# A short-convolution and pooling encoder layer on one core: the first upper gate tile loaded in whole rows and transposed on TensorE, and two tiles of the last pair exchanged in a ring of five

## Chip, core and metric

The kernel runs on one core of a Trainium2 chip, as one launch. The metric is device time in microseconds (us), lower is better. The core has five engines with instruction queues of their own, each worked through in order: PE (TensorE, matrix products; its weight loads are shown as PEld), DVE (VectorE), ACT (ScalarE), POOL (GpSimd) and SP (SyncE, which here only issues DMAs). POOL and ACT issue DMAs too.

## The reference

One layer of a streaming encoder in float32, for a prompt of 2048 frames and a sample of 32 frames, width 1024:

```python
def layer(h, p, conv_hist, pool_hist, pos, g_mix, w_in, conv_w, conv_b, pool_w, pool_scale,
          w_out, g_ple, w_ple_gate, w_ple):
    hn = rmsnorm(h, g_mix)
    proj = hn @ w_in                                             # 1024 x 3072
    hA, bA, cA, zA, vB, zB = jnp.split(proj, ..., axis=-1)       # 512 columns each
    yA, new_conv = short_conv_mixer(hA, bA, cA, zA, conv_hist, conv_w, conv_b)
    yB, new_pool = pooling_mixer(vB, zB, pool_hist, pos, pool_w, pool_scale)
    h = h + jnp.concatenate([yA, yB], axis=-1) @ w_out           # 1024 x 1024
    gate = jax.nn.sigmoid(rmsnorm(h, g_ple) @ w_ple_gate)        # 1024 x 1024
    h = h + (p @ w_ple) * gate                                   # p: 256 wide
    return h, new_conv, new_pool
# then a last rmsnorm(h, g_final)
```

The change lies in the last three of these lines: the gate product, the embedding product `p @ w_ple`, their product added to h, and the last norm.

## The kernel before

**Numbers.** A float32 operand is split into two parts, high and low (`split`: ACT casts the high part, DVE subtracts it), and a product is three PE passes of parts. Products of two tiles of 128 rows by the 1024 x 1024 weights are done in a scheme with seven half-size products instead of eight (`seven`): the operand is cut into quarters a11, a12, a21, a22, and sums of them ("frames" 11, 12, S1 to S4, 22) are multiplied by sums of the weight's quarters ("11", "T1" to "T4", "21", "22").

**Stages.** First the projection with the mixers (to about 523 us of the profile), then the product with `w_out` pair by pair of tiles (the o pairs; their results h go to DRAM as `h_d`), then the gate stage from about 705 us, which the change is in. There are 17 tiles: 16 of 128 rows and one of 32.

**The gate stage.** It begins with the late part of the embedding products (`embed`, tiles 7 to 14 and the short one; L109 and L137). For each of them SP loads an operand `pps` (256 KB), PE does two halves of six matmuls, ACT copies each half out of PSUM (`eout`, L167) and POOL stores it to `e_d`. PSUM has six banks for products (`ps_m`) and two for transposes (`ps_t`). Beside these products the weights of the gate are made into their sums (L195, L203, L210; loads `wg_b` from `g_d`), and the frames of the first pair are made (`prep_g`). Then come the eight gate pairs, `seven` for each: `carry` copies a partial product out (L1573), `out` adds, applies the sigmoid and multiplies with the tile e of `e_d` (L1579 to L1584); for most tiles POOL then adds h by an accumulating DMA (L1590); the finish (square L94, scaling L1597, store L1600) of one pair runs under the next one.

**How a tile of h gets its columns on the partitions.** The gate product needs h transposed. There are two ways. `by_quarters` loads a tile from `h_d` with four DMAs, each to 32 partitions in pieces of 1 KB, so that one DVE transpose within 32 x 32 blocks (`turned_here`, L1560) does the rest, in place; its callers pin that transpose in program order on DVE. `turned` takes a tile in whole rows, reorders its columns by two ACT copies into tiles of the ring `qa` (L1552), and transposes it by eight PE transposes into the two PSUM banks of `ps_t` (L1554); it pins nothing. Before the change only the short tile (32 rows) goes this way. Both tiles of the first pair, `first_lower` (tile 1) and `first_h` (tile 0, the upper one), are loaded by quarters. `first_h` is issued on SP behind the loads of the embedding weights (`wq`) and of the last two `wg_b`, and ahead of the `pps` of the fourth late tile and the ones after it. `prep_g(0)`'s step `second`, which makes all frames but the lower tile's, is traced behind the fifth late embedding product.

**The last pair** (`last_pair`, tiles 14 and 15) is ordered by hand: its steps are pinned with `keep_in_program_order`. Its tiles in the ring `ya` (five buffers) are one h (tile 15), one e (tile 14) and the two result tiles hg; the other h (tile 14) is in the ring `xh`, and tile 15's embedding product is made in place on PE (`e_l`). The finish of the pair before (`square1`, `scale1`, `square0`, `scale0`) runs in its steps.

**Order.** The program is traced once; a planner then orders the instructions of each engine by priority (program order) and by the time at which its own plan has them ready, gives tiles their buffers in a ring as these become free in the plan, and sets the semaphores. `keep_in_program_order` pins an instruction behind the one traced before it on its engine; `issue_after` puts a block's instructions behind a given one on its engine.

Of the kernel before, what the change touches and what calls it, by code (L numbers as in the profile page):

```python
# [36 lines left out]
def trunk(ctx, tc, x_p, x_s, c_conv, c_pool, p_p, p_s, g_mix, w_in, conv_w, conv_b, pool_w,  # L37
# [8 lines left out]
    h_d = tc.dram_tile([T, D], F32, name="h_d")  # L46
    e_d = tc.dram_tile([T, D], F32, name="e_d")
# [11 lines left out]
    def tbank(name):  # L59
        return ps_t.tile([P, 512], F32, tag="tr", name=name)  # L60
# [19 lines left out]
    def split(hi, lo, src, eng=nc.vector, later=False):  # L80
        ins = nc.scalar.copy(hi, src)  # L81
        if later:
            tc.keep_in_program_order(ins)
        eng.tensor_tensor(lo, src, hi.bitcast(F32), op=ALU.subtract)  # L84
        return ins
# [17 lines left out]
    def rows_of(pr, sa, r, n):  # L103
        return pr[r:r + n] if r < SEQ else sa
# [12 lines left out]
    def load_wp(pool, name, queue):  # L117
        wp = []
        for k in range(2):
            t = [pool.tile([P, KH, 2, P], F32R, tag="c", name=f"{name}_{k}_{h}").rearrange("p a b c -> p (a b c)")  # L120
                 for h in range(2)]
            for h in range(2):
                queue.dma_start(t[h].bitcast(F32), wl_d[k][h])
            wp.append(t)
        return wp

    def load_pps(t, i, queue, ins=False):
        n = 4 * tiles[i][1]
        load = queue.dma_start(t.rearrange("p a k n -> p (a k n)")[:, :n].bitcast(F32), pp_d[i, :, :n])
        return load if ins else t  # L130
# [251 lines left out]
    def ring4(t, name):  # L382
        return t.tile([P, D], F32, tag="t", name=name)
# [9 lines left out]
    def load_rows(pool, name, i, pr, sa=None, queue=nc.sync):  # L393
        r, n = tiles[i]
        t = ring4(pool, f"{name}_{i}")
        queue.dma_start(t[:n], pr[r:r + n] if sa is None else rows_of(pr, sa, r, n))
        return t

    with ExitStack() as s1:
# [58 lines left out]
        hn = {}  # L458
# [845 lines left out]
    with ExitStack() as s2:  # L1304
        pool = lambda name, bufs: s2.enter_context(tc.tile_pool(name=name, bufs=bufs, reuse_waits="tile"))
        qa, xh, ya, cmb = (pool(*a) for a in (("qa", 2), ("xh", 4), ("ya", 5), ("cmb", 8)))
# [79 lines left out]
        def rows_of_weight(pool, name, src, which, ks=range(KH)):  # L1386
            a = []
            for k in ks:
                a.append(ring4(pool, f"{name}_{k}") if pool is not cmb else cmb.tile([P, D], F32, tag="c", name=f"{name}_{k}"))
                ins = nc.sync.dma_start(a[-1], src[(which * KH + k) * P:(which * KH + k + 1) * P])  # L1390
            return a, ins
# [115 lines left out]
        def by_quarters(i, pool=ya):  # L1507

            r, n = tiles[i]
            t = ring4(xh if i > 3 else pool, f"hn_{i}")  # L1510
            for q in range(4):
                nc.sync.dma_start(t[q * 32:q * 32 + 32].rearrange("p (g c) -> p g c", g=4),
                                  h_d[r:r + P, q * 256:q * 256 + 256].rearrange("(g p) c -> p g c", p=32))
            return t
# [4 lines left out]
        got = {0: load_pps(ss.tile([P, 2, 2, P], F32R, tag="s", name=f"pps_{EARLY}"), EARLY, nc.sync)}  # L1519
# [8 lines left out]
            bots = rows_of_weight(cmb, "wg_b", g_d, 1, range(2))[0]  # L1528
        with tc.issue_after(embed_weight.ins):
            bots += rows_of_weight(cmb, "wg_b", g_d, 1, range(2, KH))[0]  # L1530
            first_h = by_quarters(0, xh)

        rest_e = [*range(EARLY, NT - 2), NT - 1]

# [9 lines left out]
        def turned(i, t=None):  # L1544

            r, n = tiles[i]
            t = (t or load_rows(ya, "hn", i, h_d)).rearrange("p (q k c) -> p k q c", q=4, k=KC)
            out = []
            for half in range(2):
                pt = tbank(f"pth_{i}_{half}")  # L1550
                o = qa.tile([P, KH, P], F32, tag="q", name=f"ho_{i}_{half}")
                nc.scalar.copy(o[:n].rearrange("p k (q c) -> p k q c", q=4), t[:n, half * KH:half * KH + KH])  # L1552
                for k in range(KH):
                    nc.tensor.transpose(pt[:, k * P:k * P + n], o[:n, k], ident[:n, :n])  # L1554
                out.append(pt.rearrange("p (k t) -> p k t", k=KH))
            return out

        def turned_here(t, pin=False):

            ins = nc.vector.transpose(t, t)  # L1560
            if pin:
                tc.keep_in_program_order(ins)
            u = t.rearrange("p (g k t) -> p k g t", g=4, k=KC)
            return u[:, :KH], u[:, KH:]
# [55 lines left out]
        def last_pair(i, A, square0, scale0, square1, scale1):  # L1620
# [6 lines left out]
            wp = []  # L1627
            chunk = lambda: wp.extend(load_wp(cmb, "wl", nc.sync))

            h = [load_rows(ya if b else xh, "h", i + b, h_d) for b in range(2)]  # L1630
            e = load_rows(ya, "e", i, e_d)
            tt = nc.vector.tensor_tensor
            carry, _ = gate_ops(h, [e], P, f"g{i}", i)
            hg = [ring4(ya, f"hg_{b}") for b in range(2)]
# [104 lines left out]
        def prep_g(i, ahead=False):  # L1739

            A, got = {}, {}
            whole = lambda t: t.rearrange("p k (g t) -> p k g t", g=4)

            def put(q, src, view=lambda t: t):
                A[q] = cmb.tile([P, KH, 2, P], F32R, tag="c", name=f"g{i}_{q}")
                split(view(A[q][:, :, 0]), view(A[q][:, :, 1]), src)

            def comb(q, x, y, op):
                t = whole(ss.tile([P, KH, P], F32, tag="s", name=f"g{i}_f{q}"))
                nc.vector.tensor_tensor(t, x, y, op=op)  # L1750
                return t

            lower = []

            def load():
                got["lower"] = by_quarters(i + 1) if i else first_lower
                got["upper"] = by_quarters(i) if i else first_h

            if ahead:
                load()  # L1760

            def sooner():
                if not ahead:
                    load()

            def first():
                if not got:
                    load()
                lower.extend(turned_here(got["lower"], True))

            def second():
                a21, a22 = lower
                s1 = comb("S1", a21, a22, ALU.add)
                a11, a12 = turned_here(got["upper"], True)
                put("11", a11, whole)
                s2 = comb("S2", s1, a11, ALU.subtract)
                s3 = comb("S3", a11, a21, ALU.subtract)
                put("12", a12, whole)
                put("S2", s2, whole)
                s4 = comb("S4", a12, s2, ALU.subtract)  # L1780
                put("S1", s1, whole)
                put("S3", s3, whole)
                put("S4", s4, whole)
                put("22", a22, whole)

            S[i] = A
            return {1: sooner, 2: first, 4 if i in (2, 8) else 3: second}
# [54 lines left out]
        for i in range(0, NT - 3, 2):  # L1842
            A = S.pop(i)
            following = prep_g(i + 2, not i)
            e = [load_rows(ya if i else xh, "e", i + b, e_d) for b in range(2)]
# [6 lines left out]
            if i in (0, 2, 4):  # L1852
                next(short_steps)
        last_pair(NT - 3, S[NT - 3], *finish)

# [27 lines left out]
```

## Time and profile before

| | us |
|---|---|
| median of three runs (911.08, 914.3, 911.03) | 911.08 |
| profiled execution, time | 913.21 |
| profiled execution, span of its instructions | 911.4 |
| PE busy | 889.4 |
| DVE busy | 696.0 |
| ACT busy | 452.6 |
| POOL busy | 166.8 |

The times of the table's last five rows come from one profiled execution. A row of the profile names the source line (L109 is line 109 of the kernel), the engine, the operation, what it writes and reads (`e<-wq,pps`) without buffer numbers, shapes, and a count. Rows of the timeline start with the start and the time that the merged instructions took; in brackets stands the idle time of the engine before them and what ended it. In the groups of instructions the times are least, median and largest in ns. For a DMA the first time is that of its issue; the time to its landing stands in the rows of DMA issues. Rows with SPq show the DMA queue of SP: what it issues and what it waits for. The profile's page notes that a wait for several semaphores is put down to the one that came last, and that this may be a wrong one where the engine named had long been done.

### The profile page before, as it was taken

What the parts mean: (1) busy time and instruction counts of PE and PEld (TensorE: products, weight loads), DVE (VectorE), ACT (ScalarE), POOL (GpSimd) and SP (SyncE); (2) the same over time, 40 slices, a digit from 0 to 9 for tenths busy, and PEclk for the clock granted to TensorE, in tenths of its full rate; (3) what the DMA queues carried; (4) which work ended last, traced back from release to release, by engine and by line L of the source; (5) the groups of instructions that cost most, each with busy time, mean ns of one, the idle gap of its engine ahead of it and who ended that gap; (6) DMA issues with size and microseconds to landing.
All of it is one profiled execution on the core that took longest, in us unless ns stands there. A gap on an engine that the chain in (4) does not pass through costs nothing. (4 is left out here: it accounts for less than half of the span.)

```text
span 911.4 us, 12057 instructions
## 1 busy us (share of the span) xinstructions
PE 889.4 (98%) x4110; PEld 717.0 (79%) x4110; DVE 696.0 (76%) x1140; ACT 452.6 (50%) x818; POOL 166.8 (18%) x303
## 2 busy tenths in 40 slices
PE   8999999999999999999999999999999899999996
PEld 6788888888888778877788886888887787777884
DVE  6899789897993687846767679956556967789775
ACT  7744555554453354533443365643435765446453
POOL 2210121222121023100000021211111201313322
PEclk9999999999999999999999999999999999999999
DMA  8255286857699676767744595778678784787875
GB/s 263 66 187 176 79 264 201 245 165 216 188 344 427 165 219 190 228 208 247 245 144 160 179 347 183 253 243 269 217 240 281 274 256 99 197 201 214 224 211 195
DMA packets 116843, 198.51 MB, mean 218 GB/s; under 512 B 13558, under 2 KB 74542, under 8 KB 115885
## 3 DMA queue, kind: packets, MB, share of 16 engines
q1 hardware_dynamic: 92893, 117.91, 41.1%
q0 software_dynamic: 21440, 75.44, 26.2%
q10 hardware_dynamic: 2448, 4.39, 1.3%
q8 instruction: 32, 0.52, 0.2%
q14 instruction: 30, 0.25, 0.1%
HBM read 132.53 MB, written 65.15 MB: 217 GB/s over the span
## 5 line engine op out<-in xcount | busy, mean ns | idle before, releaser
L185 PE MATMUL z_g<-wg,g_S 128*128 128x512 f32 x192 | 46.7, 392 | 2.1 <-ACT c_g L1573 2.1
L185 PE MATMUL z_o<-wo,y_S 128*128 128x512 f32 x192 | 47.4, 389 | 0.0
L185 PE MATMUL x_o<-wo_T,y_S 128*128 128x512 f32 x192 | 46.3, 390 | 0.7 <-DVE c_o L1319 0.7
L646 PE MATMUL x_zab<-B,w_zab_S 128*128 128x512 f32 x192 | 46.8, 392 | 0.2 <-DVE w_zab_S L84 0.2
L646 PE MATMUL z_zab<-B,w_zab_S 128*128 128x512 f32 x192 | 46.8, 391 | 0.0
L185 PE MATMUL x_o<-wo,y 128*128 128x512 f32 x192 | 45.2, 389 | 0.0
L185 PEld LDWEIGHTS z_g<-wg,g_S 128*128 128x128 f32 x192 | 35.7, 188 | 11.0 <-ACT c_g L1573 3.7
L646 PEld LDWEIGHTS x_zab<-B,w_zab_S 128*128 128x128 f32 x192 | 35.8, 188 | 8.9 <-DVE w_zab_S L84 0.6
L185 PEld LDWEIGHTS x_o<-wo_T,y_S 128*128 128x128 f32 x192 | 35.9, 188 | 8.6 <-DVE c_o L1319 1.2
L185 PEld LDWEIGHTS x_o<-wo,y 128*128 128x128 f32 x192 | 36.0, 188 | 7.7
L646 PEld LDWEIGHTS z_zab<-B,w_zab_S 128*128 128x128 f32 x192 | 35.8, 188 | 7.9 <-DVE w_zab_S L84 0.3
L185 PEld LDWEIGHTS z_o<-wo,y_S 128*128 128x128 f32 x192 | 36.0, 188 | 7.5
L646 PE MATMUL x_ch<-B,w_ch_S 128*128 128x512 f32 x168 | 41.9, 392 | 0.0
L646 PE MATMUL x_zbv<-B,w_zbv_S 128*128 128x512 f32 x168 | 40.9, 392 | 0.5 <-ACT zs L986 0.5
L646 PE MATMUL z_zbv<-B,w_zbv_S 128*128 128x512 f32 x168 | 40.4, 390 | 0.0
L646 PE MATMUL z_ch<-B,w_ch_S 128*128 128x512 f32 x168 | 40.4, 389 | 0.0
L646 PEld LDWEIGHTS x_zbv<-B,w_zbv_S 128*128 128x128 f32 x168 | 31.3, 188 | 8.2 <-ACT zs L986 0.9
L646 PEld LDWEIGHTS x_ch<-B,w_ch_S 128*128 128x128 f32 x168 | 31.3, 188 | 7.3 <-ACT U L986 0.4
L646 PEld LDWEIGHTS z_ch<-B,w_ch_S 128*128 128x128 f32 x168 | 31.5, 188 | 6.6
L646 PEld LDWEIGHTS z_zbv<-B,w_zbv_S 128*128 128x128 f32 x168 | 31.5, 188 | 6.5
L81 ACT CAST y_S<-y_fS 128x512 fp32r<-128x512 f32 x28 | 17.0, 619 | 27.4 <-PE x_o L185 12.0
L1373 POOL DMA_DIRECT2D gs<-in_w_ple_gate_dram x16 | 11.5, 718 | 86.7 <-DMA g_d<-gs 48.4
(554 smaller groups left out, 2272.0 us busy)
## 6 DMA issues: line engine op xcount, KB each, us to landing
wn<-in_w_in_dram SPq DMA_DIRECT2D x24, 512.0 KB, 5.1
hn<-h_d SPq DMA_DIRECT2D x65, 128.0 KB, 6.5
y<-y_d SPq DMA_DIRECT2D x16, 512.0 KB, 6.2
p_dT<-T POOLq DMA_DIRECT2D x15, 512.0 KB, 5.1
e<-e_d SPq DMA_DIRECT2D x15, 512.0 KB, 7.0
x<-in_x_prompt_dram SPq DMA_DIRECT2D x14, 512.0 KB, 5.8
e<-h_d POOLq DMA_DIRECT2D x13, 512.0 KB, 8.3
B<-p_d POOLq DMA_DIRECT2D x3, 2048.0 KB, 15.5
```

Source lines behind the costliest of these rows:

```text
L81: ins = nc.scalar.copy(hi, src)
L185: nc.tensor.matmul(ps[:n], lhs[:, k, a, :n], w[b][:, k], start=start and k + q == 0, stop=k == KH - 1 and q == 2, skip_group_check=True)
L646: nc.tensor.matmul(ps, lhs[:, k, x], b[:, k, y], start=start and k + q == 0, stop=stop and k == KH - 1 and q == 2, skip_group_check=True)
L1373: ins = nc.gpsimd.dma_start(t, rows[:, :, half * NH:half * NH + NH])
```

## The change

Three places. The first upper tile is loaded by one DMA in whole rows (`load_rows`, still into the ring `xh`), and `prep_g(0)` transposes it by `turned` instead of `turned_here`; all other tiles of the pairs stay as they were. In `last_pair` the e tile is requested ahead of the two h tiles, so in the ring of five e takes the place that the second h had, and that h the next one.

```diff
         with tc.issue_after(embed_weight.ins):
             bots += rows_of_weight(cmb, "wg_b", g_d, 1, range(2, KH))[0]
-            first_h = by_quarters(0, xh)
+            first_h = load_rows(xh, "hn", 0, h_d)
...
             chunk = lambda: wp.extend(load_wp(cmb, "wl", nc.sync))

+            e = load_rows(ya, "e", i, e_d)
             h = [load_rows(ya if b else xh, "h", i + b, h_d) for b in range(2)]
-            e = load_rows(ya, "e", i, e_d)
...
                 s1 = comb("S1", a21, a22, ALU.add)
-                a11, a12 = turned_here(got["upper"], True)
+                a11, a12 = turned_here(got["upper"], True) if i else map(whole, turned(0, got["upper"]))
                 put("11", a11, whole)
```

`turned`, which is not changed:

```python
        def turned(i, t=None):

            r, n = tiles[i]
            t = (t or load_rows(ya, "hn", i, h_d)).rearrange("p (q k c) -> p k q c", q=4, k=KC)
            out = []
            for half in range(2):
                pt = tbank(f"pth_{i}_{half}")
                o = qa.tile([P, KH, P], F32, tag="q", name=f"ho_{i}_{half}")
                nc.scalar.copy(o[:n].rearrange("p k (q c) -> p k q c", q=4), t[:n, half * KH:half * KH + KH])
                for k in range(KH):
                    nc.tensor.transpose(pt[:, k * P:k * P + n], o[:n, k], ident[:n, :n])
                out.append(pt.rearrange("p (k t) -> p k t", k=KH))
            return out
```

## The prediction

> **What bounds the kernel now.** I read the busy times and the chain first, then the stretch in which the changed tile is used, then the last pair.
>
> ```profile
> PE 889.4 (98%) x4110; PEld 717.0 (79%) x4110; DVE 696.0 (76%) x1140; ACT 452.6 (50%) x818; POOL 166.8 (18%) x303
> ...
> PE x_g L185 2%; PE z_g L185 1%; DMA e<-e_d 1%; PE y_g L185 1%; DVE hn L1560 1%; DVE e L1597 1%; PE x_g L1722 0%; DVE g_fS L1750 0%; ACT c_g L1582 0%; DVE e L1584 0%; ACT g_S L81 0%; DVE g_S L84 0%; PE e_l L109 0%; DVE c_g L1581 0%; DVE g L84 0%
> ```
>
> PE is busy for 98%, so a change pays only where PE waits or runs slowly, or behind its last product. The chain names one transfer, the last pair's e. The table by stretches, around the place where the first upper tile is used, shows the other place:
>
> ```profile
> core 0: us, PE busy (x) PEld busy (x) DVE busy (x) ACT busy (x) POOL busy (x), PEclk, DMA share, GB/s
> ...
> 713.00:717.00 4.00, 1.30 (x6) 0.79 (x5) 4.00 (x8) 3.52 (x7) 0.93 (x2) 1.00 1.02 407
> 717.00:721.00 4.00, 4.00 (x12) 3.13 (x11) 4.00 (x7) 4.00 (x9) 0.04 (x1) 0.57 0.40 160
> ```
>
> From 713 to 717 PE worked 1.30 us of 4 while the DMA engines were full (share 1.02); in the next 4 us its granted clock averaged 0.57. The timeline has the two costs:
>
> ```profile
> 705.22 8.32 PE L109 MATMUL e<-wq,pps 128*128 128x512 f32 x36
> ...
> 716.24 5.96 PE L109 MATMUL e<-wq,pps 128*128 128x512 f32 x18 [2.70 <-ACT eout L167]
> 721.80 9.93 PE L109 MATMUL e<-wq,pps 128*128 128x512 f32 x43
> 731.57 2.01 PE L137 MATMUL e<-wq,pps 128*64 128x512 f32 x8
> ...
> 715.63 0.58 ACT L167 COPY eout<-e 128x512 f32<-128x512 f32 x1
> 716.21 0.30 PEld L109 LDWEIGHTS e<-wq,pps 128*128 128x128 f32 x2 [3.09 <-ACT eout L167]
> ```
>
> Three late embedding products (12 matmuls each) ran from 705.22; PE stood still for 2.70 us ahead of the fourth. At full clock 43 matmuls took 731.57-721.80, 0.227 us each; the 17 from 716.24 up to 721.80 took 5.56 us, that is 1.70 us over 17 x 0.227. So this stretch loses 4.4 us. The wait is put down to ACT, but the weight load started at 716.21, the moment when that ACT copy ended (715.63+0.58). SP's queue names another event just before it:
>
> ```profile
> 697.25 1.75 SPq L1522 DMA_DIRECT2D wq<-wl_d  x4
> 699.04 1.04 SPq L1390 DMA_DIRECT2D wg_b<-g_d  x2
> 700.20 2.55 SPq L1512 DMA_DIRECT2D hn<-h_d  x4
> 704.40 1.62 SPq L129 DMA_DIRECT2D pps<-pp_d  x2
> ```
> ```profile
> SPq L129 <- DMA wq<-wl_d: 1.6, 1, 1.6
> ...
> SPq L129 <- DMA pps<-pp_d: 2.2, 1, 2.2
> ```
> ```profile
> L129 SPq EVENT_SEMAPHORE  x1: 1883/1883/1883, 714.2 to 714.2; - x1
> ```
>
> The hn row is the first upper tile in its four quarters; right behind it stands the pps operand that the product at 716.24 reads. It was issued at 704.40, after SP had waited 1.6 us for an older weight transfer, and a later SP wait for it lasted from 714.2 for 1.88 us, to 716.1, some 0.1 us ahead of PE's restart. I take this landing as what ended PE's wait.
>
> **Part 1, the tile in whole rows.** Removed: three of four SP issues and one DVE transpose. Added: two ACT copies and eight PE transposes. The same 0.52 MB move, in rows of 4 KB instead of pieces of 1 KB.
>
> ```profile
> DMA packets 614, 2.24 MB, mean 374 GB/s; under 512 B 69, under 2 KB 69, under 8 KB 613
> ```
> ```profile
> DMA packets 448, 0.52 MB, mean 259 GB/s; under 512 B 53, under 2 KB 411, under 8 KB 448
> ```
> ```profile
> q0 software_dynamic: 507, 1.88, 67.3%
> ```
> ```profile
> hn<-h_d SPq DMA_DIRECT2D x3, 128.0 KB, 12.8
> ```
>
> The first line is 700 to 706 us, all rows of 4 KB: 374 GB/s. The second is 707 to 709, when most of the tile's small pieces moved: 259 GB/s on full engines. So 0.52 MB cost 2.0 us and will cost 1.4: 0.6 us less. The last quarters landed 12.8 us after their issues, at about 714. From 709 to 716 (third line) POOL's stores took 67.3% of the engines and SP's loads the other third, so 0.6 us of engine time is worth about 0.6/0.33 = 1.8 us at the landing; I take 1.7. Bounds: 0, if the landing is set by the stores' turn alone, and the whole 2.70. The issue moves too, from 704.40 to about 701 (one issue instead of four, and fewer transfers ahead of it to be waited for), but the engines had a backlog from 697 on, so I count nothing for that. PE's wait becomes 1.0 us.
>
> ```profile
> 893.22 3.02 PE L185 MATMUL z_g<-wg,g_S 128*128 128x512 f32 x12 [1.65 <-ACT c_g L1573]
> 896.08 1.98 PE L185 MATMUL x_g<-wg_T,g_S 128*128 128x512 f32 x8
> ```
>
> Clock: the next-longest wait of the gate stage, 1.65 us, is followed by twelve matmuls in 896.08-893.22, 0.238 us each: no halving. So a wait of 1.0 should not lower it: -1.7 us. Bounds 0 and -1.7.
>
> Added work:
>
> ```profile
> 101.11 1.03 PE L484 MATMUL pt_g<-ident,xt 128*128 128x128 f32 x8
> ```
> ```profile
> L1560 DVE STREAM_TRANSPOSE hn<-hn x16: 1226/1238/1245, 704.2 to 870.0; 128x1024 f32<-128x1024 f32 x16
> ...
> L1552 ACT COPY ho<-hn x2: 605/611/617, 748.7 to 749.2; 32x512 f32<-32x512 f32 x2
> ```
>
> Eight 128x128 transposes of stage one took 1.03 us from the first one's start to the last one's end, a little less on PE, since the next matmul overlaps the end: +0.9 if they fall among matmuls, 0 if in what is left of the wait. I take 0.9: they are traced behind the fifth product, PE's wait is before the fourth, and no pin holds them. ACT gets 2 x 0.61 = 1.2 us where it was busy 3.52 of 4; nothing waits for it at once, as each product half has one of six PSUM banks and the copies are rows behind the reuse. If that cover were gone it would cost up to 1.2. DVE loses 1.24 us, at a place where PE did not wait for it: 0. The frame's casts and subtractions then read PSUM instead of SBUF; PE needs their results only behind the last embedding product, so whatever that changes is covered: 0.
>
> Whether transposes keep the clock up shows at the start of the kernel:
>
> ```profile
> 7.50 1.92 PE L484 MATMUL pt<-ident,xt 128*128 128x128 f32 x8
> ...
> 11.05 2.35 PE L452 MATMUL fill<-ident 128*128 128x128 f32 x20
> ```
>
> Eight took 1.92 us, 0.24 each, and twenty later ones 2.35 us, 0.12 each: the pace doubled with nothing but transposes on PE in between, so I count them as activity. [...]
>
> **Part 2, e and h change places.**
>
> ```profile
> 870.81 0.32 SPq L396 DMA_DIRECT2D h<-h_d  x1
> ...
> 884.52 0.32 SPq L396 DMA_DIRECT2D e<-e_d  x1
> ```
> ```profile
> 891.54 1.06 ACT L94 ACTIVATE junk<-e 128x1024 bf16<-128x1024 f32 x1 [2.98 <-DMA e<-h_d]
> 892.60 0.57 ACT L1573 COPY c_g<-z_g 128x512 f32<-128x512 f32 x1
> 893.10 0.69 DVE L1640 TENSOR_TENSOR c_g<-e,c_g 128x512 f32<-128x512 f32 x1 [7.08 <-DMA e<-e_d]
> ...
> 895.63 1.28 DVE L1597 SCALAR_TENSOR_TENSOR e<-e,rstd_f,g_bc 128x1024 f32<-128x1024 f32 x1
> ...
> 896.83 0.68 DVE L1677 TENSOR_TENSOR c_g<-z_g,c_g 128x512 f32<-128x512 f32 x1
> 899.65 1.70 PE L1722 MATMUL x_g<-wq,g 128*128 128x256 f32 x12 [0.24 <-DVE c_g L1677]
> 901.55 0.69 DVE L1641 TENSOR_TENSOR h<-h,c_g 128x512 f32<-128x512 f32 x1
> ```
>
> The second h of the pair had its buffer at 870.81; e got the next one at 884.52 and DVE waited 7.08 us for it. Exchanged, e is issued at 870.81, long before its first reader, and h at 884.52. If h lands like e did, just before 893.10, it is 8.4 us early for its own first reader, the row at 901.55. But PE's 1.65 us at 893.22 end with an ACT copy that stands behind the square at 891.54, which waits for POOL's accumulating transfer. That wait stays. What e frees is DVE: the scaling at 895.63 moves ahead, the addition at 896.83 starts when z_g is there (893.22+3.02 = 896.24), and PE's last wait, 0.24 us, goes. -0.2; bounds +0.2 and -0.5. On SP, a load that holds the queue until 884.52 has the pps and weight loads of this pair behind it, as e has part of them now; their reader is the product ahead of 899.65.
>
> **Sum.** -1.7 (wait) -1.7 (clock) +0.9 (transposes) -0.2 (tail) = -2.7 us. The profiled execution took 913.21 (span 911.4 and 1.8 around it), so 910.5 in its terms; the median of the runs before is 911.08, so 908.4.
>
> **Rivals.** (a) The pps landing does not move, since the stores' turn sets it: wait and slow clock stay, the transposes fall into the wait or on top: -0.2 to +0.7, about 911.3. For it: POOL's 67.3%. Against: the slow stretch of 259 GB/s ends with this change. (b) The wait shrinks, but the clock drops all the same, because PE did too few matmuls in the stretch, with or without transposes in it: -1.7+0.9-0.2 = -1.0, 910.1. For it: nothing shows where between 1.65 and 2.70 us the clock drops; against: 1.65 left it alone. [...] (c) The wait goes altogether with the transposes hidden: -2.70-1.7-0.2 = -4.6, 906.5. For it: SP stands idle 1.6 us before the pps issue and its backlog gets shorter. (d) Slower: PE takes its instructions in order, and the unpinned transposes are placed early in it, at the time at which the plan expects the tile. They then hold the embedding products back until the tile has landed (714, less 0.6) and ACT has copied it (1.2), some 714.6. Behind the third half product (18 matmuls after 705.22, 709.3) PE would then do 0.9 us of transposes and three more halves (4.1 us) and reach the product of 716.24 at 719.6: +3.4-0.2, 914.3. Behind the first half (706.6) it would be 722.3, +5.9, 917. It decides from a place ahead of the sixth half, 712.0; later there is nothing to lose. For it: the pin is gone and landing times were late in this stretch. Against: the transposes are traced behind five products that have their operands.
>
> **How the numbers follow.** Forecast 0.48, (a) 0.14, (b) 0.13, (c) 0.10, (d) 0.15. The range takes in (a), (b), (c) with some 0.5 us below it, and the nearer half of (d): 906.0 to 914.0. About 0.5% (4.6 us) is what a measurement of this kernel can tell from no change. Faster by more: half of (c) and a tail of the forecast, 0.12. Slower by more: the deeper half of (d), 0.09. Within: 0.79.
>
> **What would show it.** Right: one hn row at about 700 instead of four; PE's wait before the fourth late product at 1 us or less, and a granted clock of 1.00 from 717 to 721; eight pth transposes before 725 that wait for nothing long; the e load at about 870 and no DVE wait for it; PE's 1.65 us wait still there. Wrong: a clock below 1.00 in that stretch, a PE wait in front of pth, or new PE waits in the gate pairs for ACT or DVE that take the gain back.

## The result and the profile after

The changed kernel takes 908.93 us (median of 20 runs, 906.72 to 911.68); the kernel before, run beside it, takes 912.52 us. The ratio is 0.9963, 95% interval [0.9953, 0.9974]: 3.4 us (2.4 to 4.3) less. Run again on another chip, beside the last experiments below, the ratio was 0.9944 [0.9922, 0.9966]. The forecast was 908.4, that is 2.7 us less than the 911.08 that the kernel before had then.

The profiled execution took 910.51 us, with a span of 908.7. The page, busy times and the chain:

```profile
PE 890.5 (98%) x4118; PEld 717.2 (79%) x4118; DVE 695.5 (77%) x1139; ACT 452.6 (50%) x820; POOL 166.5 (18%) x303
...
PE z_g L185 0%; PE x_g L1722 0%; PE e_l L109 0%; PE x_g L185 0%; ACT hg L1666 0%; POOLq L1879 0%; ACT c_g L1573 0%; DVE h L1641 0%; DVE g_l L1640 0%; ACT junk L1645 0%; POOL ssq_l L1650 0%; DVEq L1640 0%; POOLq L1650 0%
```

PE has its eight matmuls more, DVE one operation less, ACT two more, and the transfer of the last pair's e has left the chain. The table by stretches, where the kernel before lost its time (the last three numbers of a row are the granted clock, the DMA share and the GB/s):

```profile
core 0: us, PE busy (x) PEld busy (x) DVE busy (x) ACT busy (x) POOL busy (x), PEclk, DMA share, GB/s
711.00:715.00 4.00, 3.07 (x14) 2.25 (x13) 3.65 (x7) 3.10 (x7) 0.53 (x1) 1.00 0.88 330
715.00:719.00 4.00, 4.00 (x19) 3.30 (x18) 4.00 (x8) 4.00 (x10) 0.65 (x2) 1.00 0.90 325
```

PE idles 0.93 us of the first stretch, and the clock is 1.00 in the second. The same place in the timeline, with SP's queue (SPq):

```profile
700.08 0.38 SPq L396 DMA_DIRECT2D hn<-h_d  x1
700.55 19.44 SPq L129 DMA_DIRECT2D pps<-pp_d  x6
704.43 8.55 PE L109 MATMUL e<-wq,pps 128*128 128x512 f32 x36
713.91 5.73 PE L109 MATMUL e<-wq,pps 128*128 128x512 f32 x24 [0.93 <-DMA pps<-pp_d]
719.48 1.03 PE L1554 MATMUL pth<-ident,ho 128*128 128x128 f32 x8
720.27 8.45 PE L109 MATMUL e<-wq,pps 128*128 128x512 f32 x36
730.41 2.90 PE L185 MATMUL x_g<-wg,g 128*128 128x512 f32 x12
```

One hn row at 700.08; the wait is 0.93 us in place of 2.70 and now carries the name of the pps transfer; the transposes stand behind the fifth product and cost 720.27 - 719.48 = 0.79 us. From the first late product to the first gate product it is 730.41 - 704.43 = 25.98 us. In the kernel before it was 733.42 - 705.22 = 28.20; its first gate product:

```profile
733.42 2.90 PE L185 MATMUL x_g<-wg,g 128*128 128x512 f32 x12
```

The last pair:

```profile
865.96 0.32 SPq L396 DMA_DIRECT2D e<-e_d  x1
879.95 0.32 SPq L396 DMA_DIRECT2D h<-h_d  x1
882.24 0.69 DVE L1640 TENSOR_TENSOR c_g<-e,c_g 128x512 f32<-128x512 f32 x1 [0.79 <-ACT c_g L1673]
887.54 1.06 ACT L94 ACTIVATE junk<-e 128x1024 bf16<-128x1024 f32 x1 [3.55 <-DMA e<-h_d]
888.60 0.56 ACT L1573 COPY c_g<-z_g 128x512 f32<-128x512 f32 x1
889.22 4.29 PE L185 MATMUL z_g<-wg,g_S 128*128 128x512 f32 x12 [2.22 <-ACT c_g L1573]
896.84 1.60 PE L1722 MATMUL x_g<-wq,g 128*128 128x256 f32 x12
```

e is requested 14 us ahead of the second h, and DVE no longer waits for it. PE still waits for the copy behind the square; here 2.22 us in place of 1.65, and this time with slow matmuls behind it: twelve in 4.29 us, where the kernel before took 3.02.

A third change was not forecast. Who PE waited for in the gate pairs, from 734 us up to the last pair (sum, times, longest), in the kernel before:

```profile
PE x_g L185 <- DVE c_g L1581: 1.6, 2, 1.0
PE x_gl L337 <- DVE c_gl L1608: 1.0, 1, 1.0
PE z_g L185 <- ACT c_g L1573: 0.4, 1, 0.4
```

and in the changed kernel:

```profile
PE x_gl L337 <- DVE c_gl L1608: 0.6, 1, 0.6
PE x_g L185 <- DVE c_g L1581: 0.6, 1, 0.6
PE z_g L185 <- ACT c_g L1573: 0.2, 1, 0.2
```

3.0 us have become 1.4. The planner, which had other work to place beside the first pair, also put the rows of PE, DVE and ACT in the following pairs in another order.

### The profile page after: what moved, and what is told of

Read it like the earlier page. It is cut to its first block, busy times and chain, and to the rows that moved or that the text cites. A ratio compares the mean times of both kernels' runs of the same rounds, so it can differ in the third digit from the quotient of the medians.

```text
span 908.7 us, 12069 instructions
## 1 busy us (share of the span) xinstructions
PE 890.5 (98%) x4118; PEld 717.2 (79%) x4118; DVE 695.5 (77%) x1139; ACT 452.6 (50%) x820; POOL 166.5 (18%) x303
## 5 line engine op out<-in xcount | busy, mean ns | idle before, releaser
L1373 POOL DMA_DIRECT2D gs<-in_w_ple_gate_dram x16 | 11.4, 716 | 87.9 <-DMA g_d<-gs 49.4
```

Of the source, the lines that this page charges most:

```text
L1373: ins = nc.gpsimd.dma_start(t, rows[:, :, half * NH:half * NH + NH])
```

## The experiments

My theory: the gain is part one's (PE waits less for the pps tile, and its clock is not halved behind that wait), part two takes a wait from DVE that PE does not feel, and what decides part one is the size of the pieces in which hn_0 moves. The rivals: the exchange carries the gain, or the count of SP's issues does; and the exchange is what lengthened the wait at the last pair.

All kernels by stage, each from one profiled execution. "Embedding" is the time from the start of the first late product to that of the first gate product; "small waits" are PE's waits over 0.15 us in the gate pairs, summed; "halved" means that the granted clock fell to 0.5 at the end of that wait or just behind it (in the kernel before from 717.30 to 720.71 us, in the changed kernel from 890.66 to 894.07, 3.41 us each); ratios stand against the kernel before on the same chip (kernels with the same letter shared a chip and its runs of the kernel before). The first late product starts anywhere from 704.0 to 708.0 us in these executions; the kernel before and part2, which are the same program up to there, start it at 705.22 and 707.14. So stages are compared here, and not whole spans.

The labels, in the order of the sections below: part1 and part2 are the two parts alone; rows4 and cols4 load the first upper tile in four transfers of rows or of columns; quart_pe uses the old transfers under the new order; after_pps and before_pps have the pps load ahead of the tile in the changed kernel and in the kernel before; sq4 stands for the squares one step later; p2_pps_sq4 is the pieces put together.

| kernel | PE's wait for pps | embedding | small waits | last pair's z_g | ratio |
|---|---|---|---|---|---|
| before | 2.70, halved | 28.20 | 3.00 | 1.65 | 1 |
| part2 (A) | 2.49, halved | 27.92 | 2.76 | 2.85, halved | 1.0006 [0.9985, 1.0027] |
| quart_pe (C) | 1.65 | 26.43 | 1.05 | 2.17, halved | 0.9957 [0.9938, 0.9977] |
| cols4 (B) | 0.74 | 25.57 | 1.37 | 1.76 | 0.9942 [0.9919, 0.9966] |
| changed | 0.93 | 25.98 | 1.43 | 2.22, halved | 0.9963 [0.9953, 0.9974] |
| changed, again (C) | 0 | 24.53 | 1.72 | 1.99 | 0.9944 [0.9922, 0.9966] |
| part1 (A) | 0.30 | 24.84 | 1.19 | 2.25, halved | 0.9946 [0.9918, 0.9974] |
| rows4 (A) | 0 | 24.55 | 1.73 | 1.94 | 0.9970 [0.9953, 0.9987] |
| after_pps (B) | 0 | 24.53 | 1.41 | 1.97, halved | 0.9948 [0.9926, 0.9970] |
| before_pps (B) | 0 | 23.61 | 0.66 | 2.97 | 0.9947 [0.9922, 0.9972] |
| after_sq4 (A) | 0 | 24.53 | 1.57 | 0 | 0.9933 [0.9912, 0.9954] |
| after_sq4, again (C) | 0 | 24.53 | 1.45 | 0 | 0.9920 [0.9898, 0.9942] |
| part1_sq4 (B) | 0 | 24.53 | 0.86 | 0 | 0.9955 [0.9937, 0.9973] |
| p2_pps_sq4 (C) | 0 | 23.61 | 1.26 | 0 | 0.9929 [0.9905, 0.9954] |

**Part one alone.** The edit against the changed kernel; the order of PE, DVE, ACT and POOL stays the same:

```diff
-            e = load_rows(ya, "e", i, e_d)
             h = [load_rows(ya if b else xh, "h", i + b, h_d) for b in range(2)]
+            e = load_rows(ya, "e", i, e_d)
```

> Part one alone (hn_0 in whole rows, turned by TensorE); the old order of the last pair's e and h stays. Theory A (the prediction's): the whole gain is part one's. PE's wait for the late pps tile goes from 2.70 us to about 0.93, the clock stays at 1.00 behind it, the transposes cost about 0.8 us, and the gate pairs start about 3 us earlier, at about 730.4. At the last pair DVE waits about 7 us for e again, yet the end comes only about 0.2 us later than with both parts: about 2 to 3 us under the kernel before. Rival B: the exchange of e and h carries the gain. Then this kernel lies within 1 us of the kernel before. Rival C: the exchange is what lengthened the wait of PE at the last pair from 1.65 to 2.22 us and halved the clock behind it. Then that wait is 1.65 us or less here, the clock stays at 1.00 there, and this kernel is about 2 us faster than the one with both parts: about 4.5 us under the kernel before.

Its timeline:

```profile
705.23 14.07 PE L109 MATMUL e<-wq,pps 128*128 128x512 f32 x60
...
887.74 0.69 DVE L1640 TENSOR_TENSOR c_g<-e,c_g 128x512 f32<-128x512 f32 x1 [7.20 <-DMA e<-e_d]
888.34 4.40 PE L185 MATMUL z_g<-wg,g_S 128*128 128x512 f32 x12 [2.25 <-ACT c_g L1573]
```

Five late products run as one row; sixty matmuls take 0.3 us more than the 13.77 they take without any wait. DVE waits 7.20 us for e again, and the ratio, 0.9946, is no worse than with both parts. Rival B falls. So does C: without the exchange PE waits as long at z_g, 2.25 us, with the slow matmuls behind it. The 0.30 us of the table is that excess of the sixty matmuls; no row shows it as a wait.

**Part two alone.** The changed kernel with `by_quarters` and `turned_here` for the first upper tile; all engines but SP keep the order of the kernel before.

```diff
-            first_h = load_rows(xh, "hn", 0, h_d)
+            first_h = by_quarters(0, xh)
...
-                a11, a12 = turned_here(got["upper"], True) if i else map(whole, turned(0, got["upper"]))
+                a11, a12 = turned_here(got["upper"], True)
```

> Part two alone (e ahead of the last pair's h tiles); hn_0 comes by four pieces of columns as before. Theory A: PE's 2.70 us wait at the late embedding and the halved clock behind it stay; DVE's wait of 7.08 us for e goes; PE still waits 1.65 us or so at the last pair's z_g. The time is that of the kernel before within 0.5 us. Rival B (the exchange carries the gain): about 2 to 3 us under the kernel before. Rival C (the exchange lengthens PE's wait at the last pair and halves the clock there, about 0.6 + 1.7 us): 1.5 to 2.5 us over the kernel before.

```profile
717.95 15.42 PE L109 MATMUL e<-wq,pps 128*128 128x512 f32 x60 [2.49 <-DMA pps<-pp_d]
...
888.23 0.69 DVE L1640 TENSOR_TENSOR c_g<-e,c_g 128x512 f32<-128x512 f32 x1 [0.79 <-ACT c_g L1673]
895.84 4.37 PE L185 MATMUL z_g<-wg,g_S 128*128 128x512 f32 x12 [2.85 <-ACT c_g L1573]
```

DVE's wait goes, PE's wait for pps stays, and the time is that of the kernel before: 1.0006. The exchange alone is worth nothing that can be measured. At z_g PE waits 2.85 us, where 1.65 was expected; that is not the exchange's doing as far as the table shows, since before_pps, without it, has 2.97.

**Four transfers of whole rows.** Only the load differs from the changed kernel; the planner keeps PE's order in this kernel and the next two, but moves a few instructions of DVE and ACT from 711.9 us on.

```diff
-            first_h = load_rows(xh, "hn", 0, h_d)
+            first_h = ring4(xh, "hn_0")
+            for q in range(4):
+                nc.sync.dma_start(first_h[q * 32:q * 32 + 32], h_d[q * 32:q * 32 + 32])
```

> The changed kernel, but hn_0 comes by four transfers of 32 rows of 4 KB each in place of one of 128 rows; TensorE still turns it. It has the number of issues of the kernel before and the row length of the kernel after. Theory A (what counts is the size of the pieces, 0.6 us of engine time over a third of the engines): SP issues the last pps loads later, but they land as in the changed kernel; PE waits about 0.9 us and the time is within 0.4 us of the changed kernel, about 3 us under the kernel before. Rival D (what counts is the number of issues ahead of the pps loads on SP, 0.64 us each, so that the pps loads are issued about 2 us later): the pps tile lands about 2 us later, PE waits about 2.5 us again, the clock is halved behind it, and the time is about 3 us over the changed kernel, that is within 1 us of the kernel before.

```profile
699.33 2.40 SPq L1533 DMA_DIRECT2D hn<-h_d  x4
702.76 15.80 SPq L129 DMA_DIRECT2D pps<-pp_d  x6
```

SP needs its four issues and sends the pps load 2.2 us later than in the changed kernel, and yet PE has no wait at all: 24.55 us of embedding. Rival D, the count of issues, falls by this trace; the times add nothing, as the ratio of 0.9970 [0.9953, 0.9987] can't be told from part one's 0.9946 on the same chip. This looked like a point for the size of the pieces, but two rows of the transfers speak against the working behind it. First the changed kernel from 706 to 708 us, then this one:

```profile
DMA packets 149, 0.53 MB, mean 265 GB/s; under 512 B 18, under 2 KB 18, under 8 KB 149
```
```profile
DMA packets 160, 0.42 MB, mean 210 GB/s; under 512 B 51, under 2 KB 51, under 8 KB 160
```

The slow stretch that the prediction put down to pieces of 1 KB (259 GB/s) is there with rows of 4 KB too, at 265 and 210 GB/s.

**Four transfers of columns.** 128 partitions with one piece of 1 KB each, TensorE as in the changed kernel.

```diff
-            first_h = load_rows(xh, "hn", 0, h_d)
+            first_h = ring4(xh, "hn_0")
+            for q in range(4):
+                nc.sync.dma_start(first_h[:, q * 256:q * 256 + 256], h_d[:P, q * 256:q * 256 + 256])
```

> The changed kernel, but hn_0 comes by four transfers of 128 rows in pieces of 1 KB, as small as in the kernel before; TensorE still turns it, and the instructions of PE, DVE and ACT keep the order of the changed kernel. Theory A (the size of the pieces decides when the pps tile lands): PE waits about 2.5 us again at the late embedding, the clock is halved behind it, and the gate pairs start at about 733, some 3 us later than in the changed kernel. Theory G (a part of the gain is the order in which the changed plan runs the gate pairs, whose small waits of PE fell from 3.0 us to 1.4 us in sum): those small waits stay at about 1.4 us whatever the load does, so this kernel keeps 1.6 us of the gain at that place and ends 1 to 2 us under the kernel before. Rival H (only what the transposes on PE change counts, not the load): no wait over 1 us at the late embedding, and the time of the changed kernel within 0.4 us, about 3.5 us under the kernel before.

```profile
702.58 3.00 SPq L1533 DMA_DIRECT2D hn<-h_d  x4
706.58 15.60 SPq L129 DMA_DIRECT2D pps<-pp_d  x6
707.02 8.36 PE L109 MATMUL e<-wq,pps 128*128 128x512 f32 x36
716.12 5.71 PE L109 MATMUL e<-wq,pps 128*128 128x512 f32 x24 [0.74 <-DMA pps<-pp_d]
```

My theory A falls here. With pieces as small as before, and the pps load issued only 0.44 us ahead of the first late product (0.82 in the kernel before), PE waits 0.74 us, less than in the changed kernel's first profile. The shorter wait does not mean that the columns land earlier than the rows. From the issue of the pps load to PE's restart it is 716.12 - 706.58 = 9.5 us here; in rows4 PE came to the same product at about 712.6 (36 matmuls of 0.227 us after 704.43) and found its operand, 9.8 us after the issue. Theory G holds: the small waits of the gate pairs, 1.37 us, go with the planned order and not with the load.

**The old transfers under the new order.**

```diff
-            first_h = load_rows(xh, "hn", 0, h_d)
+            first_h = by_quarters(0, xh)
```

> The changed kernel, but hn_0 comes by the four transfers of the kernel before, each to 32 partitions in four pieces of 1 KB for each, and TensorE turns what then lies there: the columns and rows of this one tile end up in wrong places, so the first tile's result is not the reference's. PE keeps the changed order. It differs from cols4 in the shape of the transfers alone (32 partitions with four pieces in place of 128 partitions with one). Theory K (the late landing of pps belongs to this shape): the late embedding takes 27 to 28 us up to the first gate product again (28.2 in the kernel before, 25.6 with cols4, 24.5 to 26.0 in whole rows), with a wait of PE of 2 us or more. Theory L (it belongs to the order in which the plan of the kernel before has DVE and ACT work beside it, not to the transfers): 24.5 to 26 us, with a wait under 1 us. By either the small waits of the gate pairs stay at 1.2 to 1.7 us in sum, as the changed order of PE is kept.

```profile
704.61 16.87 SPq L129 DMA_DIRECT2D pps<-pp_d  x6
715.43 5.69 PE L109 MATMUL e<-wq,pps 128*128 128x512 f32 x24 [1.65 <-ACT eout L167]
```
```profile
L129 SPq EVENT_SEMAPHORE  x1: 836/836/836, 714.5 to 714.5; - x1
```

As in the kernel before, the row names ACT, but SP's own wait for the pps tile ended at 714.5 + 0.84 = 715.3, just ahead of PE's restart. rows4, which has the same order on every engine, came to this product without any wait at 712.6, when ACT still had the sixth copy before it (from 713.51); so that copy is not what PE needs.

1.65 us and 26.43 us of embedding: between the two theories, within neither. From the issue of the pps load to PE's restart it is 10.8 us here, 11.8 in the kernel before and 11.4 in part two, against 9.5 with columns and 9.8 at most with rows4. So of the loads in four transfers the quarters look like the slow shape, by 1 to 2 us, and not by the length of their pieces. It is not shown: each is a single execution, and the changed kernel itself had waits from 0.93 to 0. How much of the microsecond between 1.65 and 2.6 belongs to DVE's and ACT's order stays open too; theirs differs from that of cols4 as well, from 715.4 us on.

**The pps load ahead of the tile**, in the changed kernel and in the kernel before. `load` is kept when it is made; the first tile is then loaded behind it.

```diff
+        pps_loads.append(load)
...
-            first_h = load_rows(xh, "hn", 0, h_d)
...
+            if c == 0:
+                with tc.issue_after(pps_loads[-1].ins):
+                    first_h = load_rows(xh, "hn", 0, h_d)      # by_quarters(0, xh) in the kernel before
```

> The changed kernel, but SP issues the fourth late pps load ahead of hn_0. Theory A: what is left of PE's wait at the late embedding (0.93 us in the profiled execution of the changed kernel, 0.3 and 0 in two others with the same order up to there) goes to 0; hn_0 lands later, at about 714, still 5 us ahead of its transposes. 0 to 0.9 us under the changed kernel. Rival I (hn_0 now lands so late that the transposes or the frames of the first pair wait): PE waits at pth or at the first gate product, and the time is up to 2 us over the changed kernel.

> The kernel before, with hn_0 by four pieces of columns and DVE's transpose as it was, but SP issues the fourth late pps load ahead of hn_0; the plan of the later gate pairs changes with it. Theory A (all that matters of part one at the late embedding is when the pps tile lands): PE's 2.70 us wait falls under 1 us and the clock stays at 1.00, without any transpose on TensorE; the gate pairs start at about 730, 3 to 4 us earlier than in the kernel before, and the time is 2 to 4 us under it, as far as the new plan's small waits leave it. Rival H (what counts is that DVE no longer turns the tile, or the transposes on PE): the wait goes but comes back at the first gate pair, where PE waits for DVE's frames; the gate pairs start within 1 us of the kernel before.

The kernel before with this edit:

```profile
707.07 21.92 PE L109 MATMUL e<-wq,pps 128*128 128x512 f32 x96
...
730.68 2.90 PE L188 MATMUL x_g<-wg,g 128*128 128x512 f32 x12
```

All eight late products in one row, no wait, with quarters of 1 KB pieces and DVE's transpose as they were. Up to 717 us PE, DVE, ACT and POOL have the order of the kernel before; only SP's differs. That shows the part of theory A that is left: the landing of pps decides PE's wait, and ACT's copy, which the profile names, does not. The embedding takes 23.61 us, 0.92 less than the 24.53 of the changed kernel without a wait; that is what TensorE's transposes cost. The ratio, 0.9947, is that of the changed kernel: a gain of the same size is to be had without whole rows. A part of it is again the planner's new order of the gate pairs, whose small waits are 0.66 us. In the changed kernel the edit leaves no wait either, and none at the transposes (rival I did not come), but there was mostly none left, and 0.9948 is no gain on 0.9944 to 0.9963.

**The squares one step later**, in the changed kernel and in part one alone.

```diff
-{1: lambda: (chunk(), square1()), 2: scale1, 3: square0, 4: lambda: (scale0(), rest()), 5: upper_half}
+{1: lambda: (chunk(), square1()), 2: scale1, 4: lambda: (square0(), scale0(), rest()), 5: upper_half}
```

> The changed kernel, but in the last pair ACT's squares of e are put one step later in its order, behind the copy c_g that PE's z_g products wait for. Theory A (PE's 2.22 us wait at the last pair is made by the square of e, which itself waits for the accumulating transfer into e, and the halved clock behind it by that wait): PE's wait there falls to 0.5 us or less, the clock stays at 1.00, and 2.2 + 1.7 = 3.9 us come free at that place; as the squares end later, DVE's scaling of e and the last store of e may take some of it back, so 2 to 4 us under the changed kernel. Rival E (the wait is not the square's: c_g is late because DVE or z_g itself is): the wait stays over 1.5 us and the time is within 0.5 us of the changed kernel. Rival F (the tail is bound by the scaling of e): the wait goes, but the time is within 0.5 us of the changed kernel or longer.

> Part one with the squares one step later in ACT's order, and the old order of the last pair's e and h. Against the changed kernel with the squares one step later it differs in nothing but the exchange. Theory A (the exchange is worth nothing only because PE stands behind the square of e anyway): here DVE waits for e until about 887.7, its scalings and the sum for z_g come about 2 us later than with the exchange, and PE waits for them at its last gate products: 1.5 to 2 us over that kernel, so about 1 us under the changed kernel. Rival J (the exchange is worth nothing in any case): the same time as that kernel within 0.5 us, 2.5 to 3 us under the changed kernel.

> The changed kernel with the squares of the last pair one step later, beside the changed kernel on one chip. The wait at the last pair's z_g is gone, so no place of it can halve the clock: 2 to 3.5 us under the changed kernel.

The changed kernel beside it, on the same chip:

> The changed kernel as it is, beside the three others on one chip. [...] Late embedding 24.5 to 26.0 us, small waits of the gate pairs 1.2 to 1.7 us, about 3.5 to 4 us under the kernel before.

The changed kernel with the edit (first run):

```profile
885.10 0.59 ACT L1573 COPY c_g<-z_g 128x512 f32<-128x512 f32 x1 [2.19 <-PE z_g L185]
885.75 3.00 PE L185 MATMUL z_g<-wg,g_S 128*128 128x512 f32 x12
886.14 1.06 ACT L94 ACTIVATE junk<-e 128x1024 bf16<-128x1024 f32 x1 [0.45 <-DMA e<-h_d]
892.28 1.70 PE L1722 MATMUL x_g<-wq,g 128*128 128x256 f32 x12 [0.35 <-DVE c_g L1677]
```

and part one alone with it:

```profile
888.19 3.00 PE L185 MATMUL z_g<-wg,g_S 128*128 128x512 f32 x12
889.97 0.69 DVE L1640 TENSOR_TENSOR c_g<-e,c_g 128x512 f32<-128x512 f32 x1 [7.16 <-ACT junk L94]
896.51 1.70 PE L1722 MATMUL x_g<-wq,g 128*128 128x256 f32 x12 [2.15 <-DVE c_g L1677]
```

The copy no longer stands behind the square, and PE's wait at z_g is gone: theory A, against E. In the changed kernel run again the wait at z_g was there, 1.99 us, and the clock behind it stayed at 1.00 (last section). On one chip the median falls from 908.98 to 906.47 us, 2.5 less, against F. The intervals of the two ratios, 0.9944 and 0.9920, overlap, but of the six runs with the edit only one, 908.25, is slower than the fastest of the six without it, 907.16. And here the exchange counts: without it, DVE's late sum for e makes PE wait 2.15 us ahead of its last gate products, with it 0.35 (0.52 in the second run). (The DVE row names ACT's square; the e that the addition reads was issued at 881.31 on SP, 8.66 us ahead of that row, as in part one alone, where the row names the transfer of e: 8.71 us, from 879.03 to 887.74.) The two kernels differ in nothing but SP's order of e and h. Only the traces show this: they ran on different chips, at 0.9955 and 0.9933 (0.9920), and the intervals of the first two overlap.

**The pieces put together** in the kernel before: pps first, e and h exchanged, squares later, no transposes on TensorE.

> The kernel before with three edits: SP issues the fourth late pps load ahead of hn_0 (which stays in quarters, turned by DVE, so there are no transposes on TensorE), e and h of the last pair change places, and the squares of the last pair come one step later. From the parts as measured one by one: 23.6 us of late embedding (0.9 less than with the transposes), gate pairs of about 155.5 us (0.7 less), the last pair as with the squares moved in the changed kernel. That is 1 to 2 us under that kernel if the parts add up, some 7 us under the kernel before; if the squares were worth something only beside the transposes, 3 to 4 us under it.

906.93 us, 0.9929, beside 906.47 on the same chip for the changed kernel with the squares moved. The embedding is at 23.61 us as expected, but PE then waits 1.15 us ahead of its last gate products instead of 0.52, and the saving does not reach the end. That is a miss of the 1 to 2 us expected. Both beat the kernel before (914.7 us there); they can't be told from each other, and p2_pps_sq4, whose interval overlaps that of the changed kernel (908.98), not from that either.

## Why the prediction was right, step by step

The size came out near the forecast (3.4 us in the first comparison, 2.7 forecast), but partly by terms that were not in the sum, and so partly by luck. The spans of the two profiled executions differ by 2.7 us too, but made up otherwise: -0.8 ahead of the first late product, where nothing was changed, -2.2 in the embedding (forecast -2.5), -1.6 in the small waits, +0.6 in the wait at z_g and +1.3 behind it, most of it the halved clock. Run again, the kernel measured -5.1.

- *PE's wait from 2.70 to 1.0 us.* The first profile had 0.93. In the executions with whole rows and the changed order of loads it was 0.93, 0.30 and five times 0; so in five of the seven the term of -1.7 was 1.0 us too small. The step that gave it, "0.52 MB cost 2.0 us and will cost 1.4", rested on a slow stretch that stays with rows of 4 KB, and columns of 1 KB left only 0.74 us. That derivation is refuted; that its result was so close to the first profile is luck. What stands is that the landing of the pps tile decides, which before_pps shows; that loads in quarters let it land later than other loads in four transfers is likely, not shown.
- *The issue's move counted at nothing.* Right as far as different loads are compared: the pps load was issued 3.88 us ahead of the first late product in the changed kernel (wait 0.93), 1.67 with four transfers of rows (0), 0.44 with columns (0.74). Within the load in one transfer it is less clear: issued 3.88 us ahead, PE waited 0.93; 4.06 ahead (part1), 0.30; 4.23 to 4.48 ahead (four executions), 0.
- *The clock, -1.7.* Right here: 1.00 behind the wait. "A wait of 1.0 should not lower it" was right too, for the wait of 0.93; over all runs the length of a wait alone did not decide (below).
- *Transposes, +0.9.* Right: 0.79 between rows, 0.92 between kernels; behind the fifth product, no wait ahead of them. Rival (d) did not come.
- *ACT and DVE, 0.* No wait of PE came of them in the embedding. But that the planner would put the later gate pairs in another order was not seen at all: some 1.5 us of small waits less, a term nearly as large as the clock's.
- *The other rivals.* (a) PE's wait got shorter, so it did not come. (b) The clock stayed up; the transposes lay among full matmuls in every kernel, so no run here tests whether they count for it. (c) The wait did go altogether in five executions, but the transposes were on the path all the same.
- *Part two, -0.2.* Right in that DVE's wait goes and the time stays. The 0.24 us ahead of the last gate products is gone in part one too, without the exchange, so no run shows the term by itself. The reason held: with the square of e out of the way, the exchange shows, by 1.6 to 1.8 us of PE's wait.
- *PE's 1.65 us at the last pair stay.* Right, and it varied: 1.65 to 2.97 us over ten executions in which the square came first. The square starts when POOL's accumulating transfer has landed, and PE's wait ends with the copy behind it (in the changed kernel the square at 887.54 us, behind 3.55 us of ACT's wait for it, the copy at 888.60, PE at 889.22). With the halved clock behind it, it gave some of the gain back in the changed kernel's profile; no run shows that as an effect of the change: the changed kernel run again has 1.99 us and no halving, and before_pps, with neither part, 2.97 us.

The mean embedding of the seven executions with whole rows in the changed order of loads is 24.8 us against 28.1 in the two with the old load and order, -3.3; with the small waits, 1.4 in the mean against 2.9, it is -4.7. The two comparisons of the changed kernel measured -3.4 and -5.1. How often the timed runs had a halving at the last pair, which by the author's estimate (half of the 3.41 us at 0.5) would move them by up to 1.7 us, is not shown.

## What to carry to other kernels

When PE stands still for an operand whose transfer is queued behind another tile's, first try to exchange the two loads: it costs a few lines, and here it did as much as a new way of loading and transposing the tile. A wait that is removed from an engine beside the path, as DVE's for e here, may be worth nothing until the wait that hides it goes too; look for what the copy that PE needs is queued behind on its engine, and move that. Where a planner orders the engines, a change in one place moves the rows of later stages: compare their waits as well before the whole difference is put down to the edit.

## What the runs showed of the hardware

The length of a wait alone did not decide whether the granted clock fell. At the last pair PE's wait of 2.17 us in quart_pe and of 2.22 us in the changed kernel had slow matmuls behind them (twelve in 4.61 and 4.29 us); behind 1.99 us in the changed kernel run again twelve took 3.02, and behind 2.97 us in before_pps eleven took 2.81. The changed kernel in its first profile, the 3.41 us ahead of the halving and the 3.41 us of it:

```profile
887.25:890.66 3.41, 1.44 (x6) 1.22 (x7) 1.02 (x1) 2.24 (x5) 1.52 (x3) 1.00 1.02 413
890.66:894.07 3.41, 3.41 (x9) 2.69 (x9) 0.78 (x2) 0.00 (x0) 1.63 (x2) 0.50 0.76 310
```

The same kernel, run again, over its wait in rows of the same length:

```profile
886.48:889.89 3.41, 1.68 (x7) 1.42 (x8) 1.26 (x1) 2.24 (x5) 1.76 (x3) 1.00 1.03 419
889.89:893.30 3.41, 3.41 (x16) 2.82 (x16) 1.27 (x3) 0.72 (x1) 1.41 (x2) 1.00 0.76 309
```

And the kernel before with pps first, whose wait of 2.97 us lies in both rows:

```profile
884.61:888.03 3.42, 2.00 (x9) 1.31 (x7) 0.00 (x0) 0.13 (x1) 0.00 (x0) 1.00 1.02 367
888.03:891.44 3.41, 1.86 (x8) 1.56 (x9) 2.56 (x4) 2.22 (x5) 1.65 (x3) 1.00 0.68 275
```

PE was idle for 1.97 us of the first row, and the clock was 0.50 in the next. In the run again it was idle for 1.73 us of the first row, in before_pps for 1.42 and 1.55 us of its two; the clock stayed at 1.00, in before_pps from 891.44 to 894.85 us as well. In the kernel before, 2.35 us idle from 713.89 to 717.30 were followed by 0.50, and 1.65 from 891.38 to 894.79 by 1.00; in quart_pe 1.65 from 712.87 to 716.28 were followed by 1.00. But in part1_sq4 1.52 us idle from 550.95 to 554.36 were followed by 0.50 from 554.36 to 557.77. So the runs show no idle time from which on the clock falls, and what decided it is not shown. The changed kernel paid about 1.7 us for it in one profiled execution (an estimate: half of the 3.41 us at 0.50) and nothing in the other. That is as much as half of what this change is worth.
